# Two output rows per partition and exps in place: a mixture-of-softmaxes kernel on one Trainium2 core

## The chip, the cores and the metric

The kernel runs on one core of a Trainium2 chip (trn2). The metric is the device time of one execution in microseconds (us). A run counts as slow when it takes over 1.5% more than the fastest of the same kernel. Before the change the median was 786.17 us (3 runs, 785.93 to 786.95).

## The reference

For each of 32 x 128 rows there are four heads of 4096 fp32 logits and four prior values. Each head is turned into a softmax, and the four softmaxes are averaged with the softmax of the prior as weights.

```python
batch, seq, vocab = 32, 128, 4096
num_heads = 4
# logits (32, 128, 4, 4096), prior (32, 128, 4), all fp32
prior_probs = softmax(prior, axis=-1)
softmax = np.exp(logits - logits.max(axis=-1, keepdims=True))
softmax = softmax / softmax.sum(axis=-1, keepdims=True)
mixture = np.sum(prior_probs[..., None] * softmax, axis=2)   # (32, 128, 4096)
```

(The prior's softmax is written out in the reference; it is shortened here. The kernels leave out the subtraction of the maximum.) 268.4 MB are read and 67.1 MB written, each byte once.

## The kernel before

One tile is one batch entry: 128 rows on 128 partitions, 64 KB of logits in each. There are two load buffers, two buffers for one head's exps, and two accumulators of one row per partition.

```python
    lpool = ctx.enter_context(tc.tile_pool(name="lpool", bufs=2))
    epool = ctx.enter_context(tc.tile_pool(name="epool", bufs=2))
    apool = ctx.enter_context(tc.tile_pool(name="apool", bufs=2))
    # ... load(0), load(1), the prior's softmax -> pp ...
    for b in range(B):
        last = b == B - 1
        inplace = b >= B - 2
        lt = ltiles.pop(b)
        # the accumulator: a tile of apool, for the last two tiles lt[:, 0]
        for h in range(H):
            et = lt[:, h] if inplace else epool.tile([P, V], FP32, name="etile")
            nc.scalar.activation(et, lt[:, h], AF.Exp, accum_out=dsum)
            # ... coeff = pp / dsum on VectorE ...
            if h == 0:
                nc.vector.tensor_scalar_mul(out=acc, in0=et, scalar1=coeff)
            elif not split:
                nc.vector.scalar_tensor_tensor(
                    out=acc, in0=et, scalar=coeff, in1=acc, op0=ALU.mult, op1=ALU.add
                )
            # ... the last head of the last tile goes in four pieces ...
        if b + 2 < B:
            load(b + 2)
        if b < B - 4:
            store(b)
        elif b == B - 3:
            store(b - 1)
            store(b)
        elif b == B - 2:
            store(b)
```

The exp (ScalarE, "ACT") writes to another buffer, so a load buffer is free once ACT has read its fourth head; VectorE ("DVE") is not waited for. And all loads and stores of the logits and the output are issued by one engine (SyncE, "SP"), in program order.

The softmax here doesn't subtract the row's maximum and nothing guards it: scores larger than these inputs give would overflow.

## Time and profile before

| | before |
|---|---|
| median time | 786.17 us |
| span of the profiled run | 784.6 us |
| DMA, share of the 16 engines' span | 99.4% |
| DVE busy, ACT busy | 70%, 60% |
| packets' sum per DMA engine at their median lengths | 776.5 us |
| longer packets (time beyond the median lengths) | 3.2 us |
| the rest (first fetch, last receipt, gaps) | 4.9 us |

The last three rows come from the trace's records of single DMA packets on the load and store queue. A packet is one contiguous run moved by one of the 16 DMA engines. A 64 KB packet took 2418 ns in median, a 16 KB one 611 and an 8 KB one 309. The sum takes every packet at one length for its size (2418, 1213, 611 or 309 ns, and 9 ns for the small packet that ends each transfer on each engine) and divides by 16. The lengths are the same for every kernel, so the sum only counts packets; what the packets really took is the sum plus "longer". Packet records overlap a little (up to 20 at once on 16 engines), so the rest is idle time less this overlap. Of the 3.2 us of longer packets, 1.4 lie in the first 50 us.

The lines from the page of the kernel before: span, busy time, the row of 40 slices for DMA (busy share in tenths), the queue's packets, bytes and share of 16 engines' span, the groups of the exp and of the scale with their waits, and the DMA issues with the median time from issue to landing.

```profile
span 784.6 us, 1001 instructions
DVE 547.3 (70%) x408; ACT 472.6 (60%) x258; POOL 0.2 (0%) x4
DMA  9999999999999999999999999999999999999997
...
q1 hardware_dynamic: 10224, 335.55, 99.4%
...
L98 ACT ACTIVATE etile<-ltile 128x4096 f32<-128x4096 f32 x120 | 433.4, 3612 | 280.8 <-DMA ltile<-in_logits_dram 241.5
...
L104 DVE TENSOR_SCALAR acc<-etile,coeff 128x4096 f32<-128x4096 f32 x30 | 70.6, 2353 | 22.1 <-DMA out_dram<-acc 22.0
...
out_dram<-acc SPq DMA_DIRECT2D x30, 2048.0 KB, 31.4
...
ltile<-in_logits_dram SPq DMA_DIRECT2D x30, 32.3
```

DMA is at 90% or more in every slice but the last. The compute engines wait for loads: of ACT's idle time, 241.5 us end with the landing of a load. A load lands 32.3 us after its issue, though its packets need only 8 x 2.418 = 19.3 us on each DMA engine. Most of the rest it stands in the queue: by the packet records its first packet starts 8.5 us after the issue (medians).

The waits of the DMA queue itself (who let SP issue, us in total, times, longest) in the kernel before:

```profile
SPq L45 <- ACT etile L98: 477.5, 30, 16.3
SPq L51 <- DVE acc L106: 150.1, 28, 5.4
```

Loads (line 45) are released by ACT's exp, stores (line 51) by DVE's accumulate. In the steady state SP issues as follows (start, length, line), from the timeline of the kernel before:

```profile
152.10 0.33 SPq L45 DMA_DIRECT2D ltile<-in_logits_dram  x1
157.87 0.34 SPq L51 DMA_DIRECT2D out_dram<-acc  x1
176.56 0.33 SPq L45 DMA_DIRECT2D ltile<-in_logits_dram  x1
```

The tile whose buffer the third line fills began its first exp at 160.51 us, 16.05 us earlier.

### The profile page before, as it was taken

What the parts mean: (1) busy time and instruction counts of PE and PEld (TensorE: products, weight loads), DVE (VectorE), ACT (ScalarE), POOL (GpSimd) and SP (SyncE); (2) the same over time, 40 slices, a digit from 0 to 9 for tenths busy, and PEclk for the clock granted to TensorE, in tenths of its full rate; (3) what the DMA queues carried; (4) which work ended last, traced back from release to release, by engine and by line L of the source; (5) the groups of instructions that cost most, each with busy time, mean ns of one, the idle gap of its engine ahead of it and who ended that gap; (6) DMA issues with size and microseconds to landing.
All of it is one profiled execution on the core that took longest, in us unless ns stands there. A gap on an engine that the chain in (4) does not pass through costs nothing.

```text
span 784.6 us, 1001 instructions
## 1 busy us (share of the span) xinstructions
DVE 547.3 (70%) x408; ACT 472.6 (60%) x258; POOL 0.2 (0%) x4
## 2 busy tenths in 40 slices
DVE  3588567866678666786667866668756687666995
ACT  0777554675546755467555676555765557755981
POOL 0000000000000000000000000000000000000000
DMA  9999999999999999999999999999999999999997
GB/s 378 428 438 451 428 428 407 452 434 421 428 423 446 457 424 434 417 427 443 428 428 435 426 455 431 435 428 416 446 428 451 431 428 426 449 428 413 428 433 307
DMA packets 10280, 335.68 MB, mean 428 GB/s; under 512 B 1152, under 2 KB 1152, under 8 KB 1184
## 3 DMA queue, kind: packets, MB, share of 16 engines
q1 hardware_dynamic: 10224, 335.55, 99.4%
q10 hardware_dynamic: 48, 0.07, 0.0%
q14 instruction: 8, 0.07, 0.0%
HBM read 268.50 MB, written 67.11 MB: 428 GB/s over the span
## 4 chain that ended last, share of the span: by engine, by line
DMA 63%; DVE 16%; ACT 13%; issue 6%; DVEq 0%; ACTq 0%; SPq 0%
DMA ltile<-in_logits_dram 59%; ACT etile L98 13%; DVE acc L106 11%; DMA out_dram<-acc 3%; DVE ltile L106 3%; DVE ltile L104 1%; DVE rden L101 1%; DVE coeff L102 1%; DVE ltile L112 0%; DVE acc L104 0%; DVEq L152 0%; ACTq L98 0%; SPq L45 0%; DVEq L104 0%
## 5 line engine op out<-in xcount | busy, mean ns | idle before, releaser
L98 ACT ACTIVATE etile<-ltile 128x4096 f32<-128x4096 f32 x120 | 433.4, 3612 | 280.8 <-DMA ltile<-in_logits_dram 241.5
L106 DVE SCALAR_TENSOR_TENSOR acc<-etile,coeff,acc 128x4096 f32<-128x4096 f32 x90 | 403.6, 4484 | 3.2
L101 DVE RECIPROCAL rden<-dsum 128x1 f32<-128x1 f32 x128 | 20.4, 160 | 186.4 <-ACT etile L98 183.3
L104 DVE TENSOR_SCALAR acc<-etile,coeff 128x4096 f32<-128x4096 f32 x30 | 70.6, 2353 | 22.1 <-DMA out_dram<-acc 22.0
L98 ACT ACTIVATE ltile<-ltile 128x4096 f32<-128x4096 f32 x8 | 28.8, 3606 | 2.5 <-DVE coeff L102 1.2
L102 DVE TENSOR_TENSOR coeff<-rden,pp 128x1 f32<-128x1 f32 x128 | 20.4, 159 | 4.4
L106 DVE SCALAR_TENSOR_TENSOR ltile<-ltile,coeff 128x4096 f32<-128x4096 f32 x5 | 22.4, 4485 | 0.2
L98 ACT ACTIVATION_READ_ACCUMULATOR etile<-ltile 128x1 f32 x120 | 22.4, 186 | 0.0
L60 DVE TENSOR_REDUCE pmax<-pr 32x128 f32<-32x512 f32 x1 | 0.7, 674 | 11.4 <-DMA pr<-in_prior_dram 11.4
L64 ACT ACTIVATE pe<-pc 32x512 f32<-32x512 f32 x1 | 0.6, 628 | 10.4 <-DVE pc L62 10.4
L112 DVE SCALAR_TENSOR_TENSOR ltile<-ltile,coeff 128x1024 f32<-128x1024 f32 x4 | 4.9, 1278 | 0.0
L104 DVE TENSOR_SCALAR ltile<-ltile,coeff 128x4096 f32<-128x4096 f32 x2 | 4.7, 2354 | 0.1
L64 ACT ACT_TABLE_LOAD x1 | 1.3, 1283 | 1.2 <-PEq L141 1.2
L78 DVE STREAM_TRANSPOSE pp<-pn 32x32 f32<-32x32 f32 x16 | 1.9, 170 | 0.1
L98 ACT ACTIVATION_READ_ACCUMULATOR ltile<-ltile 128x1 f32 x8 | 1.5, 186 | 0.0
L66 DVE TENSOR_REDUCE psum<-pe 32x128 f32<-32x512 f32 x1 | 0.7, 675 | 0.7 <-ACT pe L64 0.7
L71 DVE TENSOR_TENSOR pn<-pe,prec 32x512 f32<-32x512 f32 x1 | 1.0, 1020 | 0.0
L68 DVE RECIPROCAL prec<-psum 32x128 f32<-32x128 f32 x1 | 0.9, 942 | 0.0
L62 DVE TENSOR_TENSOR pc<-pr,pmax 32x512 f32<-32x512 f32 x1 | 0.7, 679 | 0.0
L141 POOL MEMSET const-bfloat16-1.0<- 128x1 bf16 x1 | 0.1, 101 | 0.0
L141 POOL MEMSET const-uint8-127<- 128x1 uint8 x1 | 0.1, 101 | 0.0
L141 POOL MEMSET const-float32-0.0<- 128x1 f32 x1 | 0.1, 98 | 0.2 <-issue 0.2
(1 smaller groups left out, 0.1 us busy)
## 6 DMA issues: line engine op xcount, KB each, us to landing
out_dram<-acc SPq DMA_DIRECT2D x30, 2048.0 KB, 31.4
ltile<-in_logits_dram SPq DMA_DIRECT2D x8, 2048.0 KB, 22.2
out_dram<-ltile SPq DMA_DIRECT2D x1, 2048.0 KB, 20.4
out_dram<-ltile SPq DMA_DIRECT2D x2, 1024.0 KB, 7.8
ltile<-in_logits_dram SPq DMA_DIRECT2D x30, 32.3
pr<-in_prior_dram ACTq DMA_DIRECT2D x1, 64.0 KB, 10.7
```

The lines of the kernel that those rows point to most:

```text
L60: nc.vector.reduce_max(pmax, pr, axis=AX.X)
L62: nc.vector.tensor_sub(pc, pr, pmax.unsqueeze(2).to_broadcast([B, S, H]))
L64: nc.scalar.activation(pe, pc, AF.Exp)
L68: nc.vector.reciprocal(prec, psum)
L71: nc.vector.tensor_mul(pn.rearrange("b h s -> b s h"), pe, prec.unsqueeze(2).to_broadcast([B, S, H]))
L78: nc.vector.transpose(pp[32 * t : 32 * (t + 1), h, :], pn[:, h, 32 * t : 32 * (t + 1)])
L98: nc.scalar.activation(et, lt[:, h], AF.Exp, accum_out=dsum)
L101: nc.vector.reciprocal(rden, dsum)
L102: nc.vector.tensor_mul(coeff, rden, pp[:, h, b : b + 1])
L104: nc.vector.tensor_scalar_mul(out=acc, in0=et, scalar1=coeff)
L106: nc.vector.scalar_tensor_tensor(out=acc, in0=et, scalar=coeff, in1=acc, op0=ALU.mult, op1=ALU.add)
L112: nc.vector.scalar_tensor_tensor(out=acc[:, cs], in0=et[:, cs], scalar=coeff, in1=acc[:, cs], op0=ALU.mult, op1=ALU.add,)
```

## The change

The intent: give each partition two adjacent rows of the output, so that a store moves runs of 32 KB instead of 16 KB and half as many stores are needed. The accumulators double (two of two rows); the room comes from the exp buffers, as exps are now written over the logits. Tile u is row j of pair g; a load reads one row of each partition, 64 KB every 128 KB. The first two and last three loads are cut in four, one piece per head. The core of the diff, with cuts:

```diff
+    J = 2
+    lg = logits.rearrange("b s h v -> (b s) h v").rearrange("(g p j) h v -> g j p h v", p=P, j=J)
+    ov = out.rearrange("b s v -> (b s) v").rearrange("(g p j) v -> g p j v", p=P, j=J)
...
-    epool = ctx.enter_context(tc.tile_pool(name="epool", bufs=2))
...
+        n = 1 if u < 2 or u >= U - 3 else H
+        for h in range(0, H, n):
+            nc.sync.dma_start(out=lt[:, h : h + n], in_=lg[g, j, :, h : h + n, :])
...
+        if j == 0:
+            accs[g] = apool.tile([P, J, V], FP32, name="acc")
+        acc = accs[g][:, j]
         for h in range(H):
-            et = lt[:, h] if inplace else epool.tile([P, V], FP32, name="etile")
+            et = lt[:, h]
-            nc.scalar.activation(et, lt[:, h], AF.Exp, accum_out=dsum)
+            nc.scalar.activation(et, et, AF.Exp, accum_out=dsum)
...
-        if b + 2 < B:
-            load(b + 2)
-        if b < B - 4:
-            store(b)
-        elif b == B - 3:
-            store(b - 1)
-            store(b)
-        elif b == B - 2:
-            store(b)
+        if u + 2 < U:
+            load(u + 2)
+        if j == 1 and g < G - 1:
+            store(g)
+        if u == U - 2:
+            store_part(u, 0, V)
```

More of the change, by code (lines that the diff above doesn't have):

```diff
@@ L26 @@
     P = 128
-    assert S == P and B == 32
+    J = 2
+    R = P * J
+    G = B * S // R
+    U = G * J
+    assert G * R == B * S and G <= 32
+    lg = logits.rearrange("b s h v -> (b s) h v").rearrange("(g p j) h v -> g j p h v", p=P, j=J)
+    ov = out.rearrange("b s v -> (b s) v").rearrange("(g p j) v -> g p j v", p=P, j=J)
+    pv = prior.rearrange("b s h -> (b s) h").rearrange("(g r) h -> g r h", r=R)
     lpool = ctx.enter_context(tc.tile_pool(name="lpool", bufs=2))
-    epool = ctx.enter_context(tc.tile_pool(name="epool", bufs=2))
     apool = ctx.enter_context(tc.tile_pool(name="apool", bufs=2))
@@ L33, with load @@
     cpool = ctx.enter_context(tc.tile_pool(name="cpool", bufs=1))
-    def pieces(b):
-        return 1 if b >= B - 2 else H
     ltiles = {}
-    def load(b):
+    accs = {}
+    def load(u):
         lt = lpool.tile([P, H, V], FP32, name="ltile")
-        n = pieces(b)
+        g, j = divmod(u, J)
+        n = 1 if u < 2 or u >= U - 3 else H
         for h in range(0, H, n):
-            nc.sync.dma_start(out=lt[:, h : h + n], in_=logits[b, :, h : h + n, :])
-        ltiles[b] = lt
-    accs = {}
@@ L50, in store, with store_part @@
-    def store(b, lo=0, hi=V):
-        nc.sync.dma_start(out=out[b, :, lo:hi], in_=accs[b][:, lo:hi])
+            nc.sync.dma_start(out=lt[:, h : h + n], in_=lg[g, j, :, h : h + n, :])
+        ltiles[u] = lt
+    def store(g):
+        nc.sync.dma_start(out=ov[g], in_=accs[g])
+    def store_part(u, lo, hi):
+        g, j = divmod(u, J)
+        nc.sync.dma_start(out=ov[g, :, j, lo:hi], in_=accs[g][:, j, lo:hi])
     load(0)
-    pr = cpool.tile([B, S, H], FP32, name="pr")
-    nc.scalar.dma_start(out=pr, in_=prior)
+    pr = cpool.tile([G, R, H], FP32, name="pr")
@@ L58 @@
+    nc.scalar.dma_start(out=pr, in_=pv)
     load(1)
-    pmax = cpool.tile([B, S], FP32, name="pmax")
+    pn = cpool.tile([32, H, R], FP32, name="pn")
+    nc.gpsimd.memset(pn, 0.0)
+    pmax = cpool.tile([G, R], FP32, name="pmax")
     nc.vector.reduce_max(pmax, pr, axis=AX.X)
-    pc = cpool.tile([B, S, H], FP32, name="pc")
-    nc.vector.tensor_sub(pc, pr, pmax.unsqueeze(2).to_broadcast([B, S, H]))
-    pe = cpool.tile([B, S, H], FP32, name="pe")
-    nc.scalar.activation(pe, pc, AF.Exp)
-    psum = cpool.tile([B, S], FP32, name="psum")
@@ L66 @@
-    nc.vector.reduce_sum(psum, pe, axis=AX.X)
-    prec = cpool.tile([B, S], FP32, name="prec")
-    nc.vector.reciprocal(prec, psum)
-    pn = cpool.tile([B, H, S], FP32, name="pn")
+    nc.vector.tensor_sub(pr, pr, pmax.unsqueeze(2).to_broadcast([G, R, H]))
+    nc.scalar.activation(pr, pr, AF.Exp)
+    nc.vector.reduce_sum(pmax, pr, axis=AX.X)
+    nc.vector.reciprocal(pmax, pmax)
     nc.vector.tensor_mul(
-        pn.rearrange("b h s -> b s h"), pe, prec.unsqueeze(2).to_broadcast([B, S, H])
+        pn[0:G].rearrange("g h r -> g r h"), pr, pmax.unsqueeze(2).to_broadcast([G, R, H])
@@ L73 @@
     )
-    pp = cpool.tile([P, H, B], FP32, name="pp")
-    for t in range(S // 32):
-        for h in range(H):
-            nc.vector.transpose(
-                pp[32 * t : 32 * (t + 1), h, :], pn[:, h, 32 * t : 32 * (t + 1)]
-            )
+    pq = pn.rearrange("g h (p j) -> g h p j", j=J)
+    pp = cpool.tile([P, J, H, 32], FP32, name="pp")
+    for t in range(P // 32):
+        for j in range(J):
+            for h in range(H):
+                nc.vector.transpose(
+                    pp[32 * t : 32 * (t + 1), j, h, :], pq[:, h, 32 * t : 32 * (t + 1), j]
+                )
@@ L82 @@
     NCHUNK = 4
     CW = V // NCHUNK
-    for b in range(B):
-        last = b == B - 1
-        inplace = b >= B - 2
-        lt = ltiles.pop(b)
-        if not inplace:
-            accs[b] = apool.tile([P, V], FP32, name="acc")
-        else:
-            accs[b] = lt[:, 0]
-        acc = accs[b]
+    for u in range(U):
+        g, j = divmod(u, J)
+        last = u == U - 1
+        lt = ltiles.pop(u)
+        if j == 0:
+            accs[g] = apool.tile([P, J, V], FP32, name="acc")
+        acc = accs[g][:, j]
@@ L94 @@
         for h in range(H):
-            split = last and h == H - 1
-            et = lt[:, h] if inplace else epool.tile([P, V], FP32, name="etile")
+            et = lt[:, h]
             dsum = spool.tile([P, 1], FP32, name="dsum")
-            nc.scalar.activation(et, lt[:, h], AF.Exp, accum_out=dsum)
-            coeff = spool.tile([P, 1], FP32, name="coeff")
+            nc.scalar.activation(et, et, AF.Exp, accum_out=dsum)
             rden = spool.tile([P, 1], FP32, name="rden")
             nc.vector.reciprocal(rden, dsum)
-            nc.vector.tensor_mul(coeff, rden, pp[:, h, b : b + 1])
+            coeff = spool.tile([P, 1], FP32, name="coeff")
@@ L103 @@
+            nc.vector.tensor_mul(coeff, rden, pp[:, j, h, g : g + 1])
             if h == 0:
                 nc.vector.tensor_scalar_mul(out=acc, in0=et, scalar1=coeff)
-            elif not split:
+            elif not (last and h == H - 1):
                 nc.vector.scalar_tensor_tensor(
@@ L116 @@
                     if c % 2:
-                        store(b, (c - 1) * CW, (c + 1) * CW)
-        if b + 2 < B:
-            load(b + 2)
-        if b < B - 4:
-            store(b)
-        elif b == B - 3:
-            store(b - 1)
-            store(b)
-        elif b == B - 2:
-            store(b)
+                        store_part(u, (c - 1) * CW, (c + 1) * CW)
+        if u + 2 < U:
[4 more added lines that the diff above has]
+            store_part(u, 0, V)
 _INS = ['logits', 'prior']
```

## The prediction

> **What bounds the kernel now.** DMA. The row of slices shows the 16 DMA engines 90% or more busy in 39 of 40 slices; the queue table gives the load/store queue 99.4% of the span, 335.55 MB. DVE is 70% busy, ACT 60%. The chain of waits repeats every 24.2 to 24.5 us: one 8.39 MB load (59% of the chain), then ACT and DVE releasing the next. In the trace's packet records a 64 KB packet takes 2418 ns in median, a 16 KB one 611, an 8 KB one 309: 9 ns plus 36.8 ns per KB. At those medians the packets sum to 776.5 us per engine[...]. The Trainium skill, "DMA: Bandwidth & Descriptors", section "Where 436 GB/s comes from", gives 435 GB/s as the ceiling; the trace's 27.1 x 16 = 434 agrees. Nothing but packet overhead can be saved.
>
> **What the change moves.**
> - Bytes: the same. 30 stores of 16 KB runs become 15 of 32 KB runs: by the fit 1213 ns instead of 2 x 611, 1.0 us saved per engine. Three more loads are cut in four (2444 instead of 2418 ns): +0.6 us. Net -0.4 us.
> - Exps in place: the load buffer is now released by DVE's last accumulate, not by ACT's last exp. Before, a load is issued 16 to 17 us after the landing of the tile whose buffer it takes. After: first exp 3.8 us, coefficients 0.4, 2.35 for the scale, 3 x 4.8 for the accumulates: 21 to 22 us. That is more than one load's transfer (8 x 2.42 = 19.4 us), but the two-row store (9.7 us) stands in the same queue. Taking the queue as first in, first out, loads are issued about 7 us before it runs dry (before: 8 us). So the later release is hidden, narrowly.
> - The accumulator's wait for a store (22.0 us in 28 waits) and ACT's waits for exp buffers (39 us) go away. Neither is on the DMA's path: worth nothing.
> - Start: small first loads let the first exp start near 7 us instead of 23.5. The prior's chain doubles (6.8 to 13 us), still done before the first tile's last piece. DMA is busy anyway: 0 us.
> - End: after the last landing as many bytes remain to be stored as before, and they cover the last compute: 0 us.
> - Loads step 128 KB between partitions instead of 64 KB. The same page, section "Latency and other measured facts", lists rate lost from a 512 KB pitch upwards; no run shows 128 KB yet. I expect nothing, at worst 1%.
>
> **Prediction.** 785.8 us, 80% range 783.5 to 790.0. Faster by over 2%: 0.01; within 2%: 0.95; slower by over 2%: 0.04.
>
> **What will show each step right or wrong.** The queue's share stays near 99%, about 428 GB/s. 64 KB packets stay at 2418 ns, 32 KB ones come at 1213. Loads issue on DVE's accumulate in the queue's own waits, 21 to 22 us after landing; every slice but the last is at 9. DVE's wait for stores vanishes; DVE and ACT busy times stay within 1%. The first exp starts before 10 us.
>
> **What would make it wrong.** If the queue is not served in order, or releases come 7 us later than reckoned, DMA idles once per tile: each 1 us costs 16 to 32 us in all, and slices fall below 9. If the 128 KB step or 4 MB stores slow HBM, 64 KB packets lengthen: 24 ns each would add 5 us. A faster result needs shorter packets, which the ceiling leaves no room for.

## The result, and the profile after

The changed kernel took 786.72 us in median (4 runs, 786.55 to 787.04), against 786.39 us for the kernel before in the same rounds. The ratio is 1.0004, with a 95% interval of 0.9987 to 1.0022: the same time. The outputs are right. Ratios here are the mean time of one kernel's fast runs over that of the other's of the same rounds, so not quite the ratio of the medians quoted.

| | before | after |
|---|---|---|
| span | 784.6 us | 784.8 us |
| packets' sum at median lengths | 776.5 us | 776.0 us |
| longer packets | 3.2 us | 3.5 us |
| sum and longer together | 779.7 us | 779.5 us |
| the rest | 4.9 us | 5.3 us |
| 64 KB packet, median and mean | 2418, 2430 ns | 2418, 2428 ns |
| packets of the stores of whole tiles | 16 KB, 611 ns | 32 KB, 1213 ns |
| first exp to the issue that refills its buffer | 16.05 us | 21.9 us |
| issue of a load to its first packet, first and last engine, medians | 8.5, 11.1 us | 3.1, 5.5 us |
| issue of a load to its landing, median | 32.3 us | 26.4 us |

The same lines from the page of the changed kernel:

```profile
span 784.8 us, 922 instructions
DVE 552.2 (70%) x424; ACT 467.8 (60%) x258; POOL 1.1 (0%) x5
DMA  9999999999999999999999999999999999999997
...
q1 hardware_dynamic: 9360, 335.55, 99.3%
...
L100 ACT ACTIVATE ltile<-ltile 128x4096 f32<-128x4096 f32 x128 | 461.5, 3606 | 294.2 <-DMA ltile<-in_logits_dram 288.9
...
L106 DVE TENSOR_SCALAR acc<-ltile,coeff 128x4096 f32<-128x4096 f32 x32 | 75.3, 2354 | 1.1
...
out_dram<-acc SPq DMA_DIRECT2D x15, 4096.0 KB, 35.7
...
ltile<-in_logits_dram SPq DMA_DIRECT2D x27, 26.4
```

DMA's row is the same to the last digit. DVE's 22.0 us of waits for stores are gone, and nothing came of it. What did move is the last line: loads land 26.4 us after their issue, 6 us less than before. They are no faster; they are issued later. The waits of the DMA queue in the changed kernel show who now releases them:

```profile
SPq L50 <- DVE acc L108: 683.6, 30, 31.8
```

The chain of waits of the changed kernel in the steady state (start, us, what) has the new order of events: four exps, then DVE's accumulates, then the load.

```profile
161.13 7.32 ACT ltile L100 x4
168.47 0.17 DVE rden L102
168.67 0.17 DVE coeff L104
...
168.87 4.48 DVE acc L108
...
173.65 4.48 DVE acc L108
...
178.44 4.50 DVE acc L108
...
182.99 26.64 DMA ltile<-in_logits_dram
```

From the first exp at 161.13 to the issue at 182.99 are 21.9 us. A chain like this, with 33% of the span on DVE, may be read as "DVE is on the critical path". It isn't: the chain follows issues and landings, and a load's landing is set here by what stands before it in the queue, not by its issue. Whether that holds is what the experiments have to show.

### The profile page after: what moved, and what is told of

Same layout as the page of the kernel before. It is cut to its first block, busy times and chain, and to the rows that moved or that the text cites. A ratio compares the mean times of both kernels' runs of the same rounds, so it can differ in the third digit from the quotient of the medians.

```text
span 784.8 us, 922 instructions
## 1 busy us (share of the span) xinstructions
DVE 552.2 (70%) x424; ACT 467.8 (60%) x258; POOL 1.1 (0%) x5
## 3 DMA queue, kind: packets, MB, share of 16 engines
q1 hardware_dynamic: 9360, 335.55, 99.3%
## 4 chain that ended last, share of the span: by engine, by line
DMA 51%; DVE 33%; ACT 13%; issue 1%; DVEq 0%; SPq 0%; ACTq 0%
DMA ltile<-in_logits_dram 50%; DVE acc L108 29%; ACT ltile L100 13%; DVE coeff L104 1%; DVE rden L102 1%; DMA pr<-in_prior_dram 1%; DVE acc L114 0%; DVE pp L83 0%; DVE acc L106 0%; DVE pn L74 0%; DVE pmax L73 0%; DVE pr L70 0%; DVE pmax L72 0%; DVE pmax L69 0%; DVEq L151 0%
## 5 line engine op out<-in xcount | busy, mean ns | idle before, releaser
L100 ACT ACTIVATE ltile<-ltile 128x4096 f32<-128x4096 f32 x128 | 461.5, 3606 | 294.2 <-DMA ltile<-in_logits_dram 288.9
L108 DVE SCALAR_TENSOR_TENSOR acc<-ltile,coeff,acc 128x4096 f32<-128x4096 f32 x95 | 426.0, 4484 | 3.7 <-DVE coeff L104 0.3
L106 DVE TENSOR_SCALAR acc<-ltile,coeff 128x4096 f32<-128x4096 f32 x32 | 75.3, 2354 | 1.1
L100 ACT ACTIVATION_READ_ACCUMULATOR ltile<-ltile 128x1 f32 x128 | 23.9, 187 | 0.0
L114 DVE SCALAR_TENSOR_TENSOR acc<-ltile,coeff,acc 128x1024 f32<-128x1024 f32 x4 | 4.9, 1278 | 0.0
L69 DVE TENSOR_REDUCE pmax<-pr 16x256 f32<-16x1024 f32 x1 | 1.2, 1207 | 5.0 <-DMA pr<-in_prior_dram 5.0
L72 DVE TENSOR_REDUCE pmax<-pr 16x256 f32<-16x1024 f32 x1 | 1.2, 1207 | 1.1 <-ACT pr L71 1.1
L74 DVE TENSOR_TENSOR pn<-pr,pmax 16x1024 f32<-16x1024 f32 x1 | 1.9, 1906 | 0.1
L73 DVE RECIPROCAL pmax<-pmax 16x256 f32<-16x256 f32 x1 | 1.7, 1742 | 0.0
## 6 DMA issues: line engine op xcount, KB each, us to landing
ltile<-in_logits_dram SPq DMA_DIRECT2D x27, 26.4
```

Of the source, the lines that this page charges most:

```text
L69: nc.vector.reduce_max(pmax, pr, axis=AX.X)
L73: nc.vector.reciprocal(pmax, pmax)
L74: nc.vector.tensor_mul(pn[0:G].rearrange("g h r -> g r h"), pr, pmax.unsqueeze(2).to_broadcast([G, R, H]))
L100: nc.scalar.activation(et, et, AF.Exp, accum_out=dsum)
L108: nc.vector.scalar_tensor_tensor(out=acc, in0=et, scalar=coeff, in1=acc, op0=ALU.mult, op1=ALU.add)
L114: nc.vector.scalar_tensor_tensor(out=acc[:, cs], in0=et[:, cs], scalar=coeff, in1=acc[:, cs], op0=ALU.mult, op1=ALU.add,)
```

## The experiments

The theory (the queue theory): both kernels are bound by the packets alone; the load's later release in the changed kernel is hidden because other transfers still stand in the queue. The main rival (cancelling): larger stores gain several us and the later release, or the 128 KB step of the loads, loses as many. In the table, "packets", "longer" and "rest" are the three parts of the profiled run's span as above, and "time" is the median of the fast runs.

| experiment | time | ratio to before | span | packets | longer | rest |
|---|---|---|---|---|---|---|
| changed kernel | 786.72 | 1.0004 | 784.8 | 776.0 | 3.5 | 5.3 |
| 1 store first | 852.48 | 1.0845 | 850.5 | 776.0 | 14.3 | 60.1 |
| 2 one row in place | 799.86 | 1.0174 | 798.7 | 777.2 | 6.1 | 15.3 |
| 3 16 KB stores | 787.62 | 1.0019 | 785.6 | 777.2 | 3.6 | 4.8 |
| 4 one head | 784.52 | 0.9982 | 782.7 | 776.0 | 2.6 | 4.1 |
| 5 loads in four | 791.29 | 1.0062 | 789.5 | 782.4 | 4.3 | 2.9 |
| 6 hold of 2.7 us | 797.40 | 1.0139 | 793.3 | 776.0 | 12.7 | 4.6 |
| 7 hold of 6.9 us | 847.07 | 1.0769 | 845.2 | 776.0 | 29.7 | 39.5 |
| 8 store first, loads in four | 794.72 | 1.0105 | 792.9 | 782.4 | 4.6 | 5.9 |
| 9 one row, old end | 789.43 | 1.0039 | 787.5 | 777.0 | 5.9 | 4.6 |
| 10 hold after even tiles | 797.72 | 1.0141 | 796.2 | 776.0 | 15.0 | 5.2 |
| 12 hold of 0.95 us | 789.52 | 1.0035 | 787.5 | 776.0 | 6.8 | 4.6 |

(Experiment 11 is left out of the table: its profiled run was slow.)

### 1. The store ahead of the load

```diff
-        if u + 2 < U:
-            load(u + 2)
         if j == 1 and g < G - 1:
             store(g)
+        if u + 2 < U:
+            load(u + 2)
```

> The changed kernel with two lines swapped: the two-row store is put in the queue ahead of the load that is released at the same moment. Queue theory (the new kernel is as fast because a 9.7 us store stands behind every odd load and covers the later release): now the load behind the odd tile has nothing queued ahead of it when its neighbour lands, so each pair of tiles leaves the DMA engines idle for some 4 us; reckoned with 22 us from landing to release, 19.4 us a load, 9.7 us a store and 1.2 us from issue to first packet: +60 to +80 us, 845 to 865 us, DMA share about 92%, packets as long as before. Rival (DMA is saturated whatever the order, so order and release time do not matter): 785 to 788 us.

Measured: 852.48 us, +66 us. Lines from its page (DMA's slices and the queue's share), then from its timeline of SP:

```profile
DMA  9999979899897998979989799898997979989997
...
q1 hardware_dynamic: 9360, 335.55, 92.9%
```

```profile
167.57 0.34 SPq L54 DMA_DIRECT2D out_dram<-acc  x1
168.01 19.29 SPq L50 DMA_DIRECT2D ltile<-in_logits_dram  x2
220.95 0.34 SPq L54 DMA_DIRECT2D out_dram<-acc  x1
```

A pair of tiles now takes 53.4 us (167.57 to 220.95) instead of 48.6 (in the changed kernel's chain, from the issue at 182.99 to that at 231.59). The packet records show at least half of the 16 engines idle for 4.0 to 5.2 us in each of 13 pairs, just before the store (all of them for 3.8 to 3.9 us). Nothing was added or removed but the order of two issues. With the store ahead, the odd load lands 9.7 us later, and so its tile is released later, when the queue is empty already; with the store behind, the odd tile is released while the store and the next load are still to be moved. So order and release time do matter. This is the strongest support for the queue theory, and the predicted size (+60 to +80 us) held. One part of the expectation missed: the packets did not stay as long as before. Of the 66 us, some 55 are rest and 11 are longer packets, almost all of these in the stores, whose 32 KB packets took 1301 ns in mean instead of 1213.

### 2. One row per partition, exps in place

```diff
-    J = 2
+    J = 1
...
-        if j == 1 and g < G - 1:
+        if j == J - 1 and g < G - 1:
             store(g)
-        if u == U - 2:
+        if J == 2 and u == U - 2:
             store_part(u, 0, V)
```

> The changed kernel with one row per partition instead of two: exps in place stay, the 64 KB load step and the 16 KB store runs of the kernel before come back. Queue theory: loads again are issued some 5 to 7 us before the queue runs dry, so 785 to 789 us, within 2 us of the changed kernel apart from 1 us for the shorter runs. Rival (two effects cancel: larger stores gain several us and the later release or the 128 KB step loses as many): without the larger stores the loss stands alone, 790 us or more; or, without the 128 KB step, 783 us or less.

Measured: 799.86 us, over the queue theory's range and inside the rival's. The trace tells where: the packet records show at least half of the DMA engines idle for 14.7 us in one stretch near the end (all of them for 10.5 us), and nowhere else between the start and the last receipt. Its timeline of DVE at the start of the last tile's sum, and SP's last two stores:

```profile
777.46 2.35 DVE L106 TENSOR_SCALAR acc<-ltile,coeff 128x4096 f32<-128x4096 f32 x1 [0.85 <-DMA out_dram<-acc]
779.85 9.00 DVE L108 SCALAR_TENSOR_TENSOR acc<-ltile,coeff,acc 128x4096 f32<-128x4096 f32 x2
```

```profile
791.39 2.72 SPq L58 DMA_DIRECT2D out_dram<-acc  x2
```

With two one-row accumulators the last tile needs the accumulator of tile 29, whose store stands behind the last load. DVE starts the last tile only when that store is done, and by then there is nothing left to transfer. The kernel before avoids this by summing the last two tiles in their load buffers; the changed kernel avoids it by having four rows of accumulator. My experiment had removed that, so it says nothing yet about the steady state. Experiment 9 repeats it with the old end.

### 3. The two-row store as two stores

```diff
-            store(g)
+            store_part(u - 1, 0, V)
+            store_part(u, 0, V)
```

> The changed kernel with the 4 MB store issued as two 2 MB stores, one per row, so that runs in the output are 16 KB again. Packet theory: 30 x 8 packets of 611 ns instead of 15 x 8 of 1213 ns per engine, +1.1 us in the packets' sum, 786 to 789 us. Rival (larger stores are worth several us, hidden by a loss elsewhere): over 790 us.

Measured: 787.62 us, 0.9 us over the changed kernel; the packets' sum rose by 1.2 us. Larger stores are worth about 1 us, and the rival's "several us" are not there.

### 4. Only one head is computed (wrong result)

```diff
-        for h in range(H):
+        for h in range(1):
             et = lt[:, h]
```

(The scale is used for head 0; on the last tile it is cut in four.)

> Wrong result on purpose: the changed kernel, all loads and stores kept, but only head 0 is exponentiated and scaled, so DVE work falls to about a sixth and each buffer is released 5 to 8 us after landing. If DMA alone bounds the changed kernel: 783 to 787 us, no more than 2 us under it, as the same packets have to pass. Rival (waits on compute still cost something that the gain of larger stores pays for): 5 us or more faster.

Measured: 784.52 us. From its page:

```profile
DVE 96.5 (12%) x136; ACT 121.0 (15%) x66; POOL 1.2 (0%) x5
...
q1 hardware_dynamic: 9360, 335.55, 99.5%
...
ltile<-in_logits_dram SPq DMA_DIRECT2D x27, 41.8
```

DVE is busy 96.5 us instead of 552.2, and a load's first packet now starts 19.2 us after its issue on the first engine, so the queue is never near dry. Taking away over four fifths of DVE's work gave 2.2 us between the medians, slightly over the 2 us that I had allowed. So late issues cost the changed kernel about 2 us. That a better schedule of the same transfers could hardly win more is an inference; I built no such kernel.

### 5. All loads in four pieces

```diff
-        n = 1 if u < 2 or u >= U - 3 else H
+        n = 1
```

> The changed kernel with all 32 loads cut in four by head (16 KB packets). Packet theory: 27 loads x 8 packets per engine x (4 x 611 or 613 minus 2418 = 26 to 34 ns) is 5.6 to 7.3 us, and 81 more completions of 9 ns each 0.7 us: 792 to 795 us, DMA share unchanged at 99%. Rival (16 KB packets cost nothing, since an engine's rate is what bounds): 786 to 788 us. Rival (earlier compute start lets it gain): under 786 us.

Measured: 791.29 us, +4.6 us over the changed kernel. The packets' sum rose by 6.4 us, as reckoned; 2.4 us came back in the rest (2.9 us instead of 5.3). That is not less idle time (7.5 us per engine against 7.4) but more overlap of packet records (4.7 us against 2.1). So the cost of cutting runs of 64 KB into 16 KB is real and small, just below my range of 792 to 795 us.

### 6 and 7. Holding the load buffer back

```diff
+        if u + 2 < U:
+            nc.gpsimd.memset(lt[:, H - 1, 0:3072], 0.0)      # 6; in 7: lt[:, H - 2 : H]
         if u + 2 < U:
             load(u + 2)
```

GpSimd clears part of the load tile after DVE has read it, so the refill waits for the clearing. The hold was 2.66 us per tile in experiment 6 and 6.9 us in 7 (GpSimd's added busy time over 30 tiles). DVE's busy time rose by 9.3 and 32.9 us: its scale took 2662 and 3438 ns in mean instead of 2354, which I put down to a clash with GpSimd. So the lateness is somewhat more than the hold. The clearings, from the pages of experiment 6 and 7:

```profile
L121 POOL MEMSET ltile<- 128x3072 f32 x30 | 79.7, 2657 | 666.0 <-DVE acc L108 590.4
```

```profile
L121 POOL MEMSET ltile<- 128x8192 f32 x30 | 207.8, 6925 | 590.8 <-DVE acc L108 520.1
```

> The same result, but GpSimd clears three quarters of the last head of the load tile after DVE has read it, which holds the buffer back by about 2.9 us (estimate from 941 ns for 1024 columns) before its next load. Queue theory: margin about 4.7 us (7 us less the time from issue to first packet and from last packet to landing), so hidden: 785 to 789 us. Rival (the release is on the path): +2.9 us for 16 to 30 tiles, 830 us or more. A clash of GpSimd with DVE would show as longer DVE scale operations.

> As the run before, with two heads cleared, about 7.5 us of hold. Queue theory: past the margin of about 4.7 us, DMA idles in every pair; reckoned +43 us, range +25 to +60 us: 810 to 847 us, DMA share 93 to 97%. If the margin is larger than 7.5 us: 785 to 789 us.

Measured: the longer hold cost 60 us (847.07, just past the upper end of the range). The shorter one was to be hidden and was not: its two fast runs took 795.09 and 799.71 us. Two more were over 807 and are counted as slow; the kernel before, run in the same rounds, does not scatter like this (785.41 to 787.88), so the scatter may belong to the held kernel itself, and 8 to 13 us is what the fast runs alone show. Here the queue theory in its simple form fails: leaving out the first 5 and the last 15 us, the DMA engines of experiment 6 were idle for 1.2 us per engine, against 0.2 in the changed kernel. The rows of DMA's slices, the queue and the load issues, from the pages of experiment 6 and 7 in turn:

```profile
DMA  9999999999999999999999999999999999999998
...
q1 hardware_dynamic: 9360, 335.55, 99.4%
...
ltile<-in_logits_dram SPq DMA_DIRECT2D x27, 24.4
```

```profile
DMA  9989999999999998999989899898999999989998
...
q1 hardware_dynamic: 9360, 335.55, 95.3%
...
ltile<-in_logits_dram SPq DMA_DIRECT2D x27, 23.1
```

The "busy" engines of experiment 6 moved packets that took longer. The packet records, by the place of a packet in its load (each engine moves eight 64 KB packets per load), mean ns over all odd loads, those directly ahead of the store:

```
                          1st   2nd   3rd   4th   5th   6th   7th   8th
one head     (exp. 4)    2419  2419  2419  2422  2420  2420  2422  2488
changed kernel           2428  2419  2419  2422  2419  2426  2434  2522
hold 0.95 us (exp. 12)   2470  2426  2419  2421  2419  2424  2463  2690
hold 2.7 us  (exp. 6)    2537  2439  2420  2420  2424  2419  2427  3002
hold 6.9 us  (exp. 7)    3049  2419  2419  2424  2419  2418  2419  3640
```

The last packet before the store takes 0.6 us more than the median in experiment 6 and 1.2 us more in experiment 7. With 19 us in hand (experiment 4) it is still 0.07 us longer than the median, and in the changed kernel 0.10 us, so a small part of this has nothing to do with lateness. All longer packets together rose by 9.2 us in experiment 6, which is more than its whole added span of 8.5 us.

The slack can be read from the packet records, as the time from a load's issue to its first packet. In experiment 7 the odd loads found the queue dry, and this time was 0.97 us on the first engine. What a kernel's loads take above it is the time for which they stood behind others: 8.5 - 1.0 = 7.5 us before and 3.1 - 1.0 = 2.1 us after on the first engine, and some 2.5 us more on the last (11.1 and 5.5 us in the table above). A load lands only when its last engine is done, but the queue begins to run dry with the first. From landings alone one gets more: the least time from issue to landing is about 23.1 - 1.9 (the longer packets of experiment 7) = 21.2 us, which leaves 32.3 - 21.2 = 11.1 us before and 26.4 - 21.2 = 5.2 us after. That estimate is near the slack of the last engine, and good to about 1 us.

### 8. Store first, loads in four

Experiments 1 and 5 together.

> Store ahead of the load as in the first experiment, and all loads cut in four, so that a tile's exps start with its first quarter and its release comes about 9 to 10 us after its last landing instead of 22. Queue theory: the loss of the store-first order is gone, only the packet cost of loads in four stays: within 2 us of the kernel with loads in four. If the store-first order costs for another reason than the late release (such as the store itself delaying the load): still over 830 us.

Measured: 794.72 us. Of the 66 us that the order had cost, 3.4 us are left over experiment 5, and the rest of the span explains 3.0 of them (5.9 instead of 2.9 us): near the end at least half of the DMA engines are idle for 7.1 us in one stretch, where experiment 5 has only the last 4.0 us before its last packet ends. By the order of issues, the two-row store of tiles 28 and 29 now goes ahead of the last load and no longer covers the end. I had allowed 2 us. Apart from the end, the order alone is thus harmless where tiles are released early; it was the late release that cost.

### 9. One row in place, with the old end

```diff
-            accs[g] = apool.tile([P, J, V], FP32, name="acc")
+            if u < U - 2:
+                accs[g] = apool.tile([P, J, V], FP32, name="acc")
+            else:
+                accs[g] = lt[:, 0:1]
...
-        if j == J - 1 and g < G - 1:
-            store(g)
+        if u == U - 3:
+            store(g - 1)
+        if u < U - 4 or u == U - 3 or u == U - 2:
+            store(g)
```

(On top of experiment 2; the last two loads instead of the last three are cut in four.)

> The one-row kernel with exps in place again, but with the end of the kernel before: the last two tiles are summed in their own load tile, and the stores of tiles 28 and 29 are put behind the last loads. Theory now: the 14 us that the one-row kernel lost were all at its end (its trace shows the DMA engines idle for 14.7 us there, as the last tile's sum waited for a store that stood behind the last load), and the later release of the load buffer cost it nothing: 785 to 788 us. Rival (the later release or the single rows cost something in the steady state): it stays at 795 us or more.

Measured: 789.43 us (788.77 to 790.19), 10.4 us less than experiment 2, and 3 us more than the kernel before. The end was the main loss, as the theory now had it. But it is 1.4 us over the expected range: longer packets cost 2.7 us more than in the kernel before. Part of that lies at the end (1.9 us of longer packets in the last 80 us instead of 0.2) and part between 50 us and there (3.1 us instead of 1.6). So with one row, exps in place are not quite free, and in the small the cancelling rival has a point: they cost 3 us there and 0.3 us with two rows. Shorter store runs are only some of the difference, as experiment 3 puts them at 0.9 us.

### 10, 11 and 12. Which release, and how little

The hold of 2.7 us after even tiles only, after odd tiles only, and a hold of 1024 columns (0.95 us) after all.

```diff
-        if u + 2 < U:
+        if u + 2 < U and j == 0:                              # 10; in 11: j == 1; in 12: all u
-            nc.gpsimd.memset(lt[:, H - 1, 0:3072], 0.0)
+            nc.gpsimd.memset(lt[:, H - 1, 0:3072], 0.0)      # in 12: 0:1024
```

> The changed kernel with the 2.7 us hold by GpSimd after even tiles only. The hold after all tiles cost 8 to 20 us, not by idle DMA but by a longer last packet (3.0 instead of 2.42 us) of each odd load, the one just ahead of the store. If lateness of the even tile's release (its load stands behind the store) does it: 793 us or more. If it is the odd tile's release, whose load and store go out together: 785 to 788 us.

> The hold after odd tiles only. If the odd tile's release does it, the last packets of odd loads lengthen to about 3.0 us and it takes 793 us or more; if the even one's: 785 to 788 us. If both are needed: neither run rises.

> The hold after all tiles, cut to 1024 columns (about 0.9 us). Queue theory with a margin that is simply used up: 786 to 788 us. If the changed kernel already stands at the edge, so that every bit of lateness lengthens the last packets: in proportion some 789 to 793 us.

Measured: 797.72 us for even tiles, 796.73 and 794.59 us for odd ones (its other two runs, near 810 us, were slow, and so was the profiled one, so its trace is not used). Each alone costs as much as both, so neither release is the special one. The short hold cost 2.8 us more than the changed kernel, 789.52 us (787.64 to 790.36), in line with the second of its two expectations: longer packets account for 3.3 us. The changed kernel stands at the edge: even a hold of 0.95 us was not free.

## Why the prediction was right

The time, 786.72 us, is 0.9 us over the 785.8 us predicted and inside the range. Point by point:

- **DMA bounds the kernel, and only packets count: right.** The share stayed at 99.3%. Experiment 4 shows that issuing every load 16 us earlier is worth 2.2 us.
- **Net -0.4 us of packet time: right.** The count went from 776.5 to 776.0 us, and what the packets really took from 779.7 to 779.5. 32 KB packets came at 1213 ns, as the fit said, and experiment 3 undid the saving for 1.2 us of packets and 0.9 us of time.
- **Release 21 to 22 us after landing, by DVE's accumulate: right** (21.9 us, and 683.6 us of the queue's waits).
- **Hidden by the store in the same queue: right as to the mechanism**, shown by experiment 1: with the store moved ahead of the load the same work takes 66 us longer.
- **"Loads are issued about 7 us before it runs dry (before: 8 us)": mis-sized.** From issue to first packet it was 3.1 us on the first engine and 5.5 on the last in the changed kernel, so 7 us was too much for either. Before it was 8.5 and 11.1 us, so the 8 us fits the first engine only. The change gave away some 5.5 us of the time in hand and not 1. I had reckoned as if the 16 engines moved in step. In fact the first and the last take up a load some 2.5 us apart; a release counts from the landing, which waits for the last engine, while the queue runs dry from the first.
- **"Releases come 7 us later than reckoned": the threshold was wrong, and so was its shape.** I took the slack as a step: nothing is lost until DMA idles. The runs show a slope: a hold of 0.95 us already costs 2.8 us and one of 2.7 us about 11 us, in longer packets at the ends of loads, with hardly any idle time. That it did not touch the predicted time is luck: the changed kernel stops just short of it.
- **Waits for stores and exp buffers worth nothing: right.** 22.0 us of DVE's waits disappeared, the span did not move. DVE's busy time rose by 0.9%, ACT's fell by 1.0%.
- **The start: right in time.** The first exp began at 8.62 us (I said near 7).
- **The end, "they cover the last compute: 0 us": right, but for a reason I had left out.** It also needs an accumulator that is free when the last tile comes. Experiment 2, without one, lost some 10 us there.
- **The 128 KB step: right.** 64 KB packets stayed at 2418 ns in median, and in the middle of loads also in mean.

What stays open: why a packet that ends a load takes 0.6 to 1.2 us longer when the loads are issued with little time in hand. Experiments 6, 10 and 12 show that it comes with the hold, and that a hold on either release brings it; none shows the mechanism. A clash with GpSimd's clearing at the same moment is not it in these three: none of the 208 last packets ahead of a store overlapped a clearing (in experiment 6, for instance, such packets ran from 175.5 to 180.6 us, and the clearings from 153.7 to 156.4 and from 182.8 to 185.5). In experiment 7 nearly all did overlap. Experiment 9 made the release late without GpSimd, and its longer packets between 50 us and the last 80 us rose as well, but only to 3.1 us from 1.6, where experiment 6 has 11. So a less direct part of the clearing is not ruled out.

## What to carry to other kernels

When DMA is busy in every slice, as here, cost a change by its packets first; buffers, waits and engine work were worth something in this case only where they made packets longer or left the queue idle. Before moving a buffer's release, read the time from the issue of a load to its first packet, on the engine that takes it up first: what it has above the time in an empty queue is the slack, and the order of issues in the queue can make or lose it. Don't spend that slack to the last microsecond, and check the end of the program by itself, for there the queue holds nothing to hide behind.

## What the Trainium skill lacked or had wrong

- "DMA: Bandwidth & Descriptors", "Why small descriptors are slow (HBM only)", gives a fixed cost of about 3 cycles per packet and warns of small ones. No section has the time of a single packet of 16 KB or 64 KB: here they took 611 and 2418 ns, and a straight line through the two leaves 9 ns per packet. Cutting 27 loads in four added 6.4 us to the packets' sum (completions included) and 4.6 us to the time.
- The same page, "Latency and other measured facts", lists loss of rate by row pitch from 512 KB upwards. It has no entry below that: at a step of 128 KB between partitions, runs of 64 KB come at the full 2418 ns.
- No page has it that packets can lengthen where loads are issued with little time in hand, before the queue runs dry: the last 64 KB packet of a load ahead of a store took 2.49 us with 19 us from issue to first packet, 2.52 us with 3 us, and 3.00 us when the buffer was held 2.7 us longer, with the engines still counted as 99.4% busy. A DMA busy share of 99% is thus no proof that the packets are as short as they could be.
